# RMSNorm with SiLU on one core: all transfers in one queue, in turns of loads and of stores

## The chip, the cores and the metric

The kernel runs on one of the eight cores of a Trainium2 chip; the other cores do nothing. The metric is the device time of one execution, in microseconds (us), from three runs. One further execution was recorded by the hardware profiler; all durations below come from that one.

A core has a matrix engine (TensorE, PE in the profile), a vector engine (VectorE, DVE), a scalar engine for pointwise functions (ScalarE, ACT), GpSimd (POOL) and SyncE (SP), which computes nothing and issues transfers. Transfers between the main memory (HBM) and the on-chip memory (SBUF, 128 partitions) are carried out by 16 DMA engines. A transfer is issued by an instruction on SP or on ACT, and each of the two has its own queue to those 16 engines. A transfer instruction first waits in its engine's order for whatever it needs (data computed, a buffer free), and only then goes into the queue.

## The reference

```python
def setup_inputs():
    batch, seq_len, hidden = 8, 1024, 2048
    return {
        "x": np.random.randn(batch, seq_len, hidden).astype(np.float32),
        "gamma": np.random.randn(hidden).astype(np.float32),
        "eps": np.float32(1e-5),
    }

def reference(x, gamma, eps):
    rms = np.sqrt(np.mean(x ** 2, axis=-1, keepdims=True) + eps)
    out = gamma * x / rms
    return (out * (1 / (1 + np.exp(-out)))).astype(np.float32)
```

There are 8192 rows of 2048 float32 numbers: 67.1 MB are read and 67.1 MB written.

## The kernel before

The 8192 rows are cut into 16 blocks of 512 rows. A block is a tile `xt` of 128 partitions by 4 rows (`J = 4`) of 2048, 32 KB per partition and 4.19 MB in all, and each partition's 4 rows lie next to each other in HBM, so a block is one contiguous piece of HBM (`xb`, `ob`, lines 35 and 36) and each of its 128 runs is 32 KB long. There are six such tiles (`BUFS = 6`). A block is changed in place and stored from the tile it was loaded into, so the load of block b + 6 needs the store of block b to have landed.

Per block the work is:

- squares: for each row, the sum of squares. ScalarE does some rows (`squares_scalar`, line 65, Square with a running sum), VectorE the rest (`squares_vector`, line 73). Normally they take two rows each; for the even blocks from 4 to 12 ScalarE takes one and VectorE three (`share`, line 77). The squares themselves go to PSUM tiles that nobody reads.
- `root` (line 82): ScalarE takes the root of the mean plus eps for the 4 rows. Its function needs a table load, and SiLU later needs another.
- `invert` (line 87): VectorE, the reciprocal.
- `multiply` (line 92): VectorE, x times the row's factor times gamma, four instructions, one for each row.
- `silu` (line 98): ScalarE, SiLU in place, two instructions of two rows each, and then the store (line 102).

The last block goes another way: VectorE multiplies by gamma alone (line 155) and the row's factor enters as the scale of ScalarE's SiLU (line 157), row by row.

The instructions keep the order in which the program writes them, engine by engine (`manual_schedule`). Gamma is loaded into one partition and spread to all 128 by eight matmul instructions (line 113) and a copy (line 115). For blocks 0 to 2 (`SOON`) and at the end, the multiplications of a block stand ahead of the squares of the next; in between, the squares of block b + 1 come first.

Two queues carry the transfers. Every load is issued by ACT (line 54): those of blocks 0 and 1 at once, those of 2 to 5 behind a small copy on ACT that waits for gamma (line 116), and from then on the load of block b + 3 stands behind the first square of block b + 1. Gamma and every store are issued by SP, a store when its block's SiLU is done. So from the first store on, loads and stores are in flight side by side.

Of the kernel before, what the change touches and what calls it, by code (L numbers as in the profile page):

```python
# [1 line left out]

# [4 lines left out]

ACT = mybir.ActivationFunctionType
ALU = mybir.AluOpType


@with_exitstack
def kernel(
    ctx: ExitStack,
    tc: tile.TileContext,
    x: bass.AP,
    gamma: bass.AP,
    eps: bass.AP,
    out: bass.AP,
):  # L20

    nc = tc.nc
    P = nc.NUM_PARTITIONS
    f32 = mybir.dt.float32
    x2 = x.flatten_outer_dims()
    o2 = out.flatten_outer_dims()  # L30
    n, d = x2.shape
    J = 4
    BUFS = 6
    nblk = n // (P * J)
    xb = x2.rearrange("(b p j) d -> b p (j d)", p=P, j=J)
    ob = o2.rearrange("(b p j) d -> b p (j d)", p=P, j=J)

    singles = ctx.enter_context(tc.tile_pool(name="singles", bufs=1))
    pool = ctx.enter_context(tc.tile_pool(name="pool", bufs=BUFS))
    small = ctx.enter_context(tc.tile_pool(name="small", bufs=2))  # L40
    psum = ctx.enter_context(tc.tile_pool(name="psum", bufs=1, space=bass.MemoryType.PSUM))

    Q = 4
    w = d // Q
    g = singles.tile([P, d], f32)
    eps_t = singles.tile([P, 1], f32)
    ones = singles.tile([P, P], f32)
    junk_a = psum.tile([P, d], f32, name="junk_a")
    junk_v = psum.tile([P, d], f32, name="junk_v")
    blocks, sss, rmss, rstds = {}, {}, {}, {}  # L50

    def load(b):
        xt = pool.tile([P, J * d], f32, name="xt")
        nc.scalar.dma_start(out=xt, in_=xb[b])  # L54
        blocks[b] = xt

    def row(b, j):
        return blocks[b][:, j * d:(j + 1) * d]

    def squares_scalar(b, loads=()):  # L60


        sss[b] = small.tile([P, J], f32, name="ss")
        for j in range(share(b)):
            nc.scalar.activation(out=junk_a, in_=row(b, j), func=ACT.Square,  # L65
                                 accum_out=sss[b][:, j:j + 1])
            if j == 0:
                for s in loads:
                    load(s)

    def squares_vector(b):
        for j in range(share(b), J):
            nc.vector.tensor_tensor_reduce(  # L73
                out=junk_v, in0=row(b, j), in1=row(b, j), scale=1.0, scalar=0.0,
                op0=ALU.mult, op1=ALU.add, accum_out=sss[b][:, j:j + 1])

    def share(b):
        return 1 if 4 <= b <= 12 and b % 2 == 0 else 2

    def root(b):  # L80
        rms = small.tile([P, J], f32, name="rms")
        nc.scalar.activation(out=rms, in_=sss.pop(b), func=ACT.Sqrt, scale=1.0 / d, bias=eps_t)  # L82
        rmss[b] = rms

    def invert(b):
        rstd = small.tile([P, J], f32, name="rstd")
        nc.vector.reciprocal(out=rstd, in_=rmss.pop(b))  # L87
        rstds[b] = rstd

    def multiply(b):  # L90
        for j in range(J):
            nc.vector.scalar_tensor_tensor(out=row(b, j), in0=row(b, j), scalar=rstds[b][:, j:j + 1],  # L92
                                           in1=g, op0=ALU.mult, op1=ALU.mult)

    def silu(b):
        for h in range(0, J, 2):
            cols = slice(h * d, (h + 2) * d)
            nc.scalar.activation(out=blocks[b][:, cols], in_=blocks[b][:, cols], func=ACT.Silu)  # L98
        store(b)

    def store(b):
        nc.sync.dma_start(out=ob[b], in_=blocks[b])

    with tc.manual_schedule():

        load(0)
        nc.vector.memset(ones, 1.0)  # L107
        nc.vector.memset(eps_t, float(eps))
        nc.scalar.activation(out=junk_a[:, 0:1], in_=ones[:, 0:1], func=ACT.Square)  # L109
        nc.sync.dma_start(out=g[0:1, :], in_=bass.AP(tensor=gamma.tensor, offset=gamma.offset, ap=[[d, 1], [1, d]]))  # L110
        for c in range(Q):
            cols = slice(c * w, (c + 1) * w)
            nc.tensor.matmul(junk_v[:, cols], ones[0:1, :], g[0:1, cols], start=True, stop=True)  # L113
        load(1)
        nc.vector.tensor_copy(out=g, in_=junk_v)  # L115
        nc.scalar.copy(out=junk_a[:, 0:1], in_=junk_v[:, d - 1:d])  # L116
        for b in range(2, BUFS):
            load(b)

        last = nblk - 1
        SOON = 3
        squares_scalar(0)
        squares_vector(0)
        root(0)
        invert(0)
        for b in range(last):
            loads = [b + 3] if BUFS <= b + 3 < nblk else []
            if b < SOON:  # L130
                multiply(b)
                squares_scalar(b + 1, loads)
                silu(b)
                squares_vector(b + 1)
                root(b + 1)
            elif b < last - 1:
                squares_scalar(b + 1, loads)
                squares_vector(b + 1)
                root(b + 1)
                multiply(b)  # L140
                silu(b)
            else:
                multiply(b)
                squares_scalar(b + 1)
                silu(b)
                squares_vector(b + 1)
                root(b + 1)
            if b + 1 < last:
                invert(b + 1)


        for j in range(J):
            if j == J // 2:
                invert(last)
            nc.vector.tensor_mul(out=row(last, j), in0=row(last, j), in1=g)  # L155
        for j in range(J):
            nc.scalar.activation(out=row(last, j), in_=row(last, j), func=ACT.Silu,  # L157
                                 scale=rstds[last][:, j:j + 1])
        store(last)


# [1 line left out]
_INS = ['x', 'gamma', 'eps']  # L163
_OUTS = [((8, 1024, 2048), 'float32')]

_NUMBERS = {'eps': 9.999999747378752e-06}


# [26 lines left out]
```

## Time and profile before

| what | value |
|---|---|
| time, median of 3 runs | 317.0 us (316.79 to 317.33) |
| span of the profiled execution | 315.1 us |
| VectorE busy | 235.3 us, 75% of the span |
| ScalarE busy | 213.9 us, 68% |
| TensorE busy | 7.2 us, 2% |
| loads: 16 issues of 4096 KB | median 38.7 us from issue to landing |
| stores: 16 issues of 4096 KB | median 29.0 us from issue to landing |
| SP waiting for SiLU (line 98) ahead of a store | 271.4 us in 15 waits, the longest 22.2 |
| VectorE's squares waiting for a load | 42.2 us in 11 waits |

The span runs from the first to the last instruction of the profiled execution; the times of the runs include what lies around it. In the profile a group's row has the line, the engine, the operation, what is written from what, the shapes and the count, and behind the bars the busy time in us, the mean of one in ns, the idle time of the engine just before these instructions and what ended it. A row on a stretch of time has its start and end, its length, each engine's busy time, the clock, and last the busy share of the 16 DMA engines and the GB/s they moved. A DMA packet is counted where it starts, so short stretches can show a share over 1. The page's digits are tenths in 40 equal slices of 7.88 us.

### The profile page before, as it was taken

What the parts mean: (1) busy time and instruction counts of PE and PEld (TensorE: products, weight loads), DVE (VectorE), ACT (ScalarE), POOL (GpSimd) and SP (SyncE); (2) the same over time, 40 slices, a digit from 0 to 9 for tenths busy, and PEclk for the clock granted to TensorE, in tenths of its full rate; (3) what the DMA queues carried; (4) which work ended last, traced back from release to release, by engine and by line L of the source; (5) the groups of instructions that cost most, each with busy time, mean ns of one, the idle gap of its engine ahead of it and who ended that gap; (6) DMA issues with size and microseconds to landing.
All of it is one profiled execution on the core that took longest, in us unless ns stands there. A gap on an engine that the chain in (4) does not pass through costs nothing.

```text
span 315.1 us, 439 instructions
## 1 busy us (share of the span) xinstructions
PE 7.2 (2%) x8; PEld 2.5 (1%) x8; DVE 235.3 (75%) x157; ACT 213.9 (68%) x137; POOL 0.2 (0%) x4
## 2 busy tenths in 40 slices
PE   6200000000000000000000000000000000000000
PEld 2000000000000000000000000000000000000000
DVE  0679697979895695957969489593995939999600
ACT  1269998972799258682687827877278768779910
POOL 0000000000000000000000000000000000000000
DMA  8999999999999999999999999999999999999997
GB/s 334 412 453 416 383 458 408 462 403 462 403 459 408 454 412 458 408 462 403 462 403 462 408 458 408 458 408 458 416 449 416 449 416 449 428 437 428 437 428 308
DMA packets 4613, 134.24 MB, mean 426 GB/s; under 512 B 514, under 2 KB 514, under 8 KB 514
## 3 DMA queue, kind: packets, MB, share of 16 engines
q10 hardware_dynamic: 2304, 67.11, 49.8%
q1 hardware_dynamic: 2306, 67.12, 49.3%
q14 instruction: 3, 0.02, 0.0%
HBM read 67.12 MB, written 67.11 MB: 426 GB/s over the span
## 4 chain that ended last, share of the span: by engine, by line
DMA 68%; DVE 14%; ACT 11%; issue 1%; ACTq 1%; DVEq 0%
DMA xt<-in_x_dram 68%; DVE xt L92 9%; DVE junk_v L73 5%; ACT xt L98 4%; ACT junk_a L65 3%; ACT xt L157 2%; ACT L82 1%; ACTq L190 1%; ACT L157 0%; ACT L98 0%; ACT rms L82 0%; DVE ss L73 0%; ACTq L54 0%; DVE rstd L87 0%; ACT L109 0%
## 5 line engine op out<-in xcount | busy, mean ns | idle before, releaser
L92 DVE SCALAR_TENSOR_TENSOR xt<-xt,rstd,g 128x2048 f32<-128x2048 f32 x60 | 137.0, 2346 | 0.1
L98 ACT ACTIVATE xt<-xt 128x4096 f32<-128x4096 f32 x30 | 108.3, 3615 | 27.4 <-DVE xt L92 27.4
L73 DVE CUSTOM_DVE_ANT_0 junk_v<-xt 128x2048 f32<-128x2048 f32 x37 | 85.1, 2299 | 42.9 <-DMA xt<-in_x_dram 42.2
L65 ACT ACTIVATE junk_a<-xt 128x2048 f32<-128x2048 f32 x27 | 50.7, 1876 | 16.1 <-DMA xt<-in_x_dram 14.0
L82 ACT ACT_TABLE_LOAD x15 | 19.2, 1283 | 26.6 <-DVE ss L73 26.5
L98 ACT ACT_TABLE_LOAD x14 | 18.0, 1283 | 0.2
L115 DVE COPY g<-junk_v 128x2048 f32<-128x2048 f32 x1 | 2.3, 2292 | 9.0 <-PE junk_v L113 9.0
L87 DVE RECIPROCAL rstd<-rms 128x4 f32<-128x4 f32 x16 | 2.7, 172 | 8.4 <-ACT rms L82 8.4
L155 DVE TENSOR_TENSOR xt<-xt,g 128x2048 f32<-128x2048 f32 x4 | 8.9, 2277 | 0.0
L82 ACT ACTIVATE rms<-ss,eps_t 128x4 f32<-128x4 f32 x16 | 4.8, 297 | 5.7 <-DVE ss L73 5.5
L157 ACT ACTIVATE xt<-xt,rstd 128x2048 f32<-128x2048 f32 x4 | 7.7, 1991 | 0.0
L113 PE MATMUL junk_v<-g,ones 1*128 1x512 f32 x8 | 7.2, 1072 | 2.8 <-DMA g<-in_gamma_dram 2.8
L116 ACT COPY junk_a<-junk_v 128x1 f32<-128x1 f32 x1 | 0.1, 144 | 9.8 <-DVE g L115 9.8
L73 DVE DVE_READ_ACCUMULATOR2_ANT ss<- 128x1 f32 x37 | 5.2, 141 | 0.0
L65 ACT ACTIVATION_READ_ACCUMULATOR junk_a<-xt 128x1 f32 x27 | 5.0, 186 | 0.0
L113 PEld LDWEIGHTS junk_v<-g,ones 1*128 1x128 f32 x8 | 2.5, 325 | 5.9 <-issue 5.9
L109 ACT ACT_TABLE_LOAD x1 | 1.3, 1283 | 1.1 <-PEq L176 1.1
L157 ACT ACT_TABLE_LOAD x1 | 1.3, 1283 | 0.0
L107 DVE MEMSET ones<- 128x128 f32 x1 | 0.2, 165 | 0.8 <-PEq L176 0.8
L109 ACT ACTIVATE junk_a<-ones 128x1 f32<-128x1 f32 x1 | 0.2, 174 | 0.0
L176 POOL MEMSET const-bfloat16-1.0<- 128x1 bf16 x1 | 0.1, 103 | 0.0
L176 POOL MEMSET const-uint8-127<- 128x1 uint8 x1 | 0.1, 102 | 0.0
(3 smaller groups left out, 0.3 us busy)
## 6 DMA issues: line engine op xcount, KB each, us to landing
xt<-in_x_dram ACTq DMA_DIRECT2D x16, 4096.0 KB, 38.7
out_dram<-xt SPq DMA_DIRECT2D x16, 4096.0 KB, 29.0
g<-in_gamma_dram SPq DMA_DIRECT2D x1, 8.0 KB
```

The source lines that it names most:

```text
L65: nc.scalar.activation(out=junk_a, in_=row(b, j), func=ACT.Square, accum_out=sss[b][:, j:j + 1])
L73: nc.vector.tensor_tensor_reduce(out=junk_v, in0=row(b, j), in1=row(b, j), scale=1.0, scalar=0.0, op0=ALU.mult, op1=ALU.add, accum_out=sss ...
L82: nc.scalar.activation(out=rms, in_=sss.pop(b), func=ACT.Sqrt, scale=1.0 / d, bias=eps_t)
L87: nc.vector.reciprocal(out=rstd, in_=rmss.pop(b))
L92: nc.vector.scalar_tensor_tensor(out=row(b, j), in0=row(b, j), scalar=rstds[b][:, j:j + 1], in1=g, op0=ALU.mult, op1=ALU.mult)
L98: nc.scalar.activation(out=blocks[b][:, cols], in_=blocks[b][:, cols], func=ACT.Silu)
L109: nc.scalar.activation(out=junk_a[:, 0:1], in_=ones[:, 0:1], func=ACT.Square)
L113: nc.tensor.matmul(junk_v[:, cols], ones[0:1, :], g[0:1, cols], start=True, stop=True)
L115: nc.vector.tensor_copy(out=g, in_=junk_v)
L155: nc.vector.tensor_mul(out=row(last, j), in0=row(last, j), in1=g)
L157: nc.scalar.activation(out=row(last, j), in_=row(last, j), func=ACT.Silu, scale=rstds[last][:, j:j + 1])
L190: with _tile.TileContext(nc) as tc:
```

## The change

All 32 block transfers are issued by SP, in an order written out by hand (`QUEUE`). It alternates between turns of one direction: 6 blocks in, 5 out, 5 in, 5 out, 5 in, 6 out. Gamma's load moves from SP's queue to ACT's; the small copy of line 116 goes.

The six tiles become one tile `ring` with six slots, block b in slot b % 6. Two neighbouring blocks 2q and 2q + 1 now share their stretch of HBM: of the 8 rows that lie next to each other, a partition takes the first 4 for the even block and the last 4 for the odd one (`view`). So a single block has 128 runs of 32 KB, spaced by 64 KB, and a pair taken in one transfer has 128 runs of 64 KB. Pairs are taken in one transfer four times: the load of 4 and 5, and the stores of 0 and 1, 6 and 7, 10 and 11. A paired store waits for the SiLU of both.

`transfers(done)` issues the list's next entries for as long as they are loads or stores of blocks up to `done`. SP itself waits, in this order, for whatever each entry needs.

The compute order follows the turns (`GROUPS`: blocks 0 to 5, 6 to 10, 11 to 15). In the middle of a group the squares of block b + 1 come ahead of the multiplications of block b; a group's last block (but for the very last) is squared only after the multiplications and SiLU of the one before. ScalarE and VectorE now take two rows of squares each in every block.

```diff
+QUEUE = [
+    ('L', 0), ('L', 1), ('L', 2), ('L', 3), ('L', 4, 5),
+    ('S', 0, 1), ('S', 2), ('S', 3), ('S', 4),
+    ('L', 6), ('L', 7), ('L', 8), ('L', 9), ('L', 10),
+    ('S', 5), ('S', 6, 7), ('S', 8), ('S', 9),
+    ('L', 11), ('L', 12), ('L', 13), ('L', 14), ('L', 15),
+    ('S', 10, 11), ('S', 12), ('S', 13), ('S', 14), ('S', 15),
+]
+
+GROUPS = [range(0, 6), range(6, 11), range(11, 16)]
...
-    BUFS = 6
+    SLOTS = 6
...
-    xb = x2.rearrange("(b p j) d -> b p (j d)", p=P, j=J)
-    ob = o2.rearrange("(b p j) d -> b p (j d)", p=P, j=J)
...
-    pool = ctx.enter_context(tc.tile_pool(name="pool", bufs=BUFS))
-    small = ctx.enter_context(tc.tile_pool(name="small", bufs=2))
+    small = ctx.enter_context(tc.tile_pool(name="small", bufs=3))
...
+    ring = singles.tile([P, SLOTS * J * d], f32, name="xt")
...
-    def load(b):
-        xt = pool.tile([P, J * d], f32, name="xt")
-        nc.scalar.dma_start(out=xt, in_=xb[b])
-        blocks[b] = xt
+    def rows(b, j, k):
+        at = (b % SLOTS) * J + j
+        return ring[:, at * d:(at + k) * d]
...
+    def view(t, blocks):
+
+        q = blocks[0] // 2
+        both = t[q * 2 * P * J:(q + 1) * 2 * P * J, :].rearrange("(p j) d -> p (j d)", p=P, j=2 * J)
+        at = blocks[0] % 2 * J
+        return both[:, at * d:(at + len(blocks) * J) * d]
+
+    todo = list(QUEUE)
+
+    def transfer():
+        kind, *blocks = todo.pop(0)
+        sb = rows(blocks[0], 0, len(blocks) * J)
+        if kind == "L":
+            nc.sync.dma_start(out=sb, in_=view(x2, blocks))
+        else:
+            nc.sync.dma_start(out=view(o2, blocks), in_=sb)
+
+    def transfers(done):
+
+        while todo and (todo[0][0] == "L" or todo[0][-1] <= done):
+            transfer()
...
-    def share(b):
-        return 1 if 4 <= b <= 12 and b % 2 == 0 else 2
+    def squares(b):
+        squares_scalar(b)
+        squares_vector(b)
+        root(b)
...
-        store(b)
-
-    def store(b):
-        nc.sync.dma_start(out=ob[b], in_=blocks[b])
+            nc.scalar.activation(out=rows(b, h, 2), in_=rows(b, h, 2), func=ACT.Silu)
+        transfers(b)
...
-        load(0)
+        transfer()
...
+        nc.scalar.dma_start(out=g[0:1, :], in_=bass.AP(tensor=gamma.tensor, offset=gamma.offset, ap=[[d, 1], [1, d]]))
...
-        nc.sync.dma_start(out=g[0:1, :], in_=bass.AP(tensor=gamma.tensor, offset=gamma.offset, ap=[[d, 1], [1, d]]))
...
-        load(1)
+        transfer()
         nc.vector.tensor_copy(out=g, in_=junk_v)
-        nc.scalar.copy(out=junk_a[:, 0:1], in_=junk_v[:, d - 1:d])
-        for b in range(2, BUFS):
-            load(b)
...
+        transfers(-1)
+
+        for group in GROUPS:
+            first, end = group[0], group[-1]
+            squares(first)
+            invert(first)
+            multiply(first)
+            squares_scalar(first + 1)
+            silu(first)
+            squares_vector(first + 1)
+            root(first + 1)
+            for b in group[1:-1]:
+                if b + 1 < end or end == last:
+                    squares(b + 1)
+                invert(b)
                 multiply(b)
                 silu(b)
...
+            if end < last:
+                squares(end)
+                invert(end)
+                multiply(end)
+                silu(end)
...
-        store(last)
+        transfers(last)
```

## The prediction

> **What bounds the kernel now.** I read the page's DMA rows first, because a kernel that reads 67 MB, writes 67 MB and does little arithmetic is likely to be held by its transfers.
>
> ```profile
> span 315.1 us, 439 instructions
> DMA  8999999999999999999999999999999999999997
> GB/s 334 412 453 416 383 458 408 462 403 462 403 459 408 454 412 458 408 462 403 462 403 462 408 458 408 458 408 458 416 449 416 449 416 449 428 437 428 437 428 308
> DMA packets 4613, 134.24 MB, mean 426 GB/s; under 512 B 514, under 2 KB 514, under 8 KB 514
> q10 hardware_dynamic: 2304, 67.11, 49.8%
> q1 hardware_dynamic: 2306, 67.12, 49.3%
> ```
>
> The DMA digits are 9 in all slices but the first and the last, and the two queues together occupy 99.1% of the 16 engines' time (q10 is the loads, q1 the stores and gamma). So the span is bytes divided by rate, plus the two ends. The GB/s digits swing because a packet of 32 KB is counted whole where it starts. To see the rate I asked for longer stretches, cut where the traffic changes: start, loads alone, the first store's arrival, loads and stores together, stores alone, end. The last two columns are the share of the DMA engines and GB/s.
>
> ```profile
> 0.00:1.70 1.70, 0.00 (x0) 0.00 (x0) 0.17 (x2) 0.56 (x1) 0.20 (x4) 1.00 0.03 5
> 1.70:3.40 1.70, 0.62 (x1) 0.49 (x2) 0.00 (x0) 0.90 (x2) 0.00 (x0) 1.00 1.03 308
> 3.40:36.00 32.60, 6.54 (x8) 1.99 (x6) 20.95 (x14) 18.97 (x15) 0.00 (x0) 1.00 1.01 434
> 36.00:40.00 4.00, 0.00 (x0) 0.00 (x0) 3.17 (x3) 3.96 (x5) 0.00 (x0) 1.00 1.09 377
> 40.00:280.00 240.00, 0.00 (x0) 0.00 (x0) 194.53 (x129) 168.71 (x105) 0.00 (x0) 1.00 1.00 433
> 280.00:310.33 30.33, 0.00 (x0) 0.00 (x0) 16.46 (x11) 20.79 (x13) 0.00 (x0) 1.00 1.00 433
> ```
>
> This is the central reading. Loads alone run at 434 GB/s, loads and stores interleaved at 433, stores alone at 433. Mixing the directions, which the change stops, costs nothing here. At 433 GB/s the 134.24 MB take 310.0 us (the rounding of 433 is worth 0.4), and a block of 4.19 MB 9.69 us.
>
> What is left are two places where packets are long. At 1.70 to 3.40 the engines are busy 1.03 × 1.70 = 1.75 us at 308/1.03 = 299 GB/s, so 1.75 × (1 − 299/433) = **0.54 us** is lost while the first packets fill the path. At 36 to 40, where the first store joins (it is issued at 35.18), they are busy 1.09 × 4 = 4.36 us at 377/1.09 = 346 GB/s: 4.36 × (1 − 346/433) = **0.88 us** lost. Sum: 1.70 idle before the first load packet, 0.54, 0.88 and 310.0 make 313.1; the remaining 2.0 us to 315.1 are the last landing, the closing and the rounding. The profiled span stands 1.9 us below the median of 317.0; I take that as fixed and add it to every span.
>
> The compute engines' rows give the prices needed below; at 235 and 214 us busy neither VectorE nor ScalarE is the bound.
>
> ```profile
> L92 DVE SCALAR_TENSOR_TENSOR xt<-xt,rstd,g 128x2048 f32<-128x2048 f32 x60 | 137.0, 2346 | 0.1
> L98 ACT ACTIVATE xt<-xt 128x4096 f32<-128x4096 f32 x30 | 108.3, 3615 | 27.4 <-DVE xt L92 27.4
> L73 DVE CUSTOM_DVE_ANT_0 junk_v<-xt 128x2048 f32<-128x2048 f32 x37 | 85.1, 2299 | 42.9 <-DMA xt<-in_x_dram 42.2
> L82 ACT ACT_TABLE_LOAD x15 | 19.2, 1283 | 26.6 <-DVE ss L73 26.5
> L82 ACT ACTIVATE rms<-ss,eps_t 128x4 f32<-128x4 f32 x16 | 4.8, 297 | 5.7 <-DVE ss L73 5.5
> L155 DVE TENSOR_TENSOR xt<-xt,g 128x2048 f32<-128x2048 f32 x4 | 8.9, 2277 | 0.0
> ```
>
> **The change, part by part.**
>
> *Bytes and start.* All 67.11 MB each way stay: 310.0 us at 433 GB/s. The first load is issued by SP instead of ACT; both queues issue their first transfer at 0.73 in the trace, so the 1.70 and the 0.54 stay. Gamma changes places with it on ACT's queue; ACT has only its table load behind it. The L116 copy, which held the loads of blocks 2 to 5 back to 12.4 us, goes; since 434 GB/s flow across that point, its removal is worth 0.
>
> *One queue instead of two.* In the new list SP waits on each store's SiLU and on each slot's earlier store, in order, and everything behind it in the list waits too. This costs nothing as long as the DMA queue still holds issued transfers. The stock at each point: loads 0 to 5 end at 1.70 + 0.54 + 6 × 9.69 = 60.4. The pair of stores 0,1 needs SiLU of block 1. The trace has that block's squares and root done by 36.8; the new order puts block 2's squares, root and table load on ACT before SiLU (about 2 × 2.03 + 0.30 + 2 × 1.28 = 6.9, to 43.7), while VectorE does two squares (2 × 2.4) and four multiplies (9.14) from 34.0 to about 48.1; the second SiLU half of 3.6 ends it at 51.7. **Margin 8.7 us.** In the second group, block 6 lands near 119 (60.4 + 5 stores + itself = 118.5, and 0.5 to land); squares 4.8, root, table load and inverse 1.8, multiplies 9.14, squares of 7 and 8 9.6, multiplies 9.14, SiLU 3.6 give 157.1 for the pair 6,7, against 60.4 + 11 × 9.69 = 167.0, when loads 6 to 10 and store 5 are through. **Margin 9.9 us.** In the third, block 11 lands near 215.9 (22 blocks); the same chain without the pair's second multiply, with ScalarE's own order, reaches SiLU of 11 at about 238, against 60.4 + 20 × 9.69 = 254.2. Margin 16. The last store: from 215.9 VectorE has 10 squares × 2.4, 16 multiplies × 2.29, 4 × 2.24 and one 1.8 wait = 71.4, to 287.3, and two last SiLU rows (2 × 1.9) make 291, against 60.4 + 25 × 9.69 = 302.7. Margin 11. Loads that wait for a store: load 10 waits for store 4 (landed at about 109.4) with loads 6 to 9, 38.8 us of work, in front of it; load 15 likewise. So no turn runs dry, and the compute order (GROUPS, the dropped `share`) costs 0 under this cover. If cover failed, the price is the shortfall plus a refill: 0.97 from issue to first packet (0.73 to 1.70) and 0.54.
>
> *The first store's stretch.* 0.88 us were lost when a second queue joined a running one. In the new kernel the first store follows in a queue that is already running. Bounds: 0 (it belongs to the store, and stays) to 0.88 gained. The only other such stretch, 0.54, is also a queue that starts; later stores begin on a queue with work left (29.0 us median from issue to landing against 9.69 of work) and the stretch from 40 on shows no loss. Nearer to that: I take **−0.9**.
>
> *Five turns of direction inside one queue.* No row shows one. Bounds: the stretch 40 to 280, where 433 GB/s flow while each engine's packets alternate between queues, gives 0 per turn; the one entry of a new direction gives 0.88. A gain below zero is excluded by 434 for loads alone. The alternating stretch has thousands of changes of direction and the entry one, so I take **0** each and keep 5 × 0.88 = 4.4 for the range.
>
> *64 KB runs.* Four pairs × 128 partitions merge 512 packets: 32 fewer on each of 16 engines, and 4 fewer completions. The nearest row is the completion packet of 4 B, 9 ns in the DMA records: at most 36 × 9 ns = 0.32 gained, 0 if a run is still cut at 32 KB; middle: **−0.15**. That blocks 4 and 5 land together delays block 4's squares by 9.69, inside the margins above (store 4 is ready near 89, needed at 98.5).
>
> The Trainium skill, DMA: Bandwidth & Descriptors, section "Why small descriptors are slow (HBM only)", gives about 3 cycles per packet beside one cycle per 32 B; on that, an estimate of the merged packets' gain is 3 of 2051 cycles on a quarter of the bytes, near 0.1 us, inside my bounds. A rule on the same page speaks against the change: "Latency and other measured facts" has rates falling with power-of-two row pitch in HBM (207 against 214 GB/s per direction at 512 KiB). The change doubles the pitch of the 32 KB runs from 32 to 64 KB; no row here shows a wider pitch, and if that 3% held for the 24 unpaired blocks, an estimate from the page is 0.033 × 0.75 × 310 = 8 us more.
>
> **Sum**: 315.1 − 0.9 − 0.15 + 0 = 314.05 of span, and with 1.9, **316.0 us**.
>
> **The rivals.**
>
> 1. *The stretch moves with the first store.* For: both lossy places come where bytes first go a new way. Against: the other one has loads alone. Then only the 64 KB gain is left: 317.0 − 0.15 = 316.85, within what can be told from no change.
> 2. *Each turn costs what the first store cost* (slower). Between two queues, one queue's next packet is ready while the other's finishes; in one queue a write stands directly behind a read, and the pipe may fill anew. For: the only first change of direction shown cost 0.88. Against: 433 in the alternating stretch. At the full price 317.0 − 0.88 − 0.15 + 5 × 0.88 = 320.4. It decides from 5t > 0.9 + 0.15 + 0.63, t = 0.34 us a turn.
> 3. *A turn runs dry*: the ring is one tile, and if its slots were ordered as a whole, or a margin of 8.7 were eaten, SP would issue late. For: SP's long waits in the old trace were for SiLU, and loads now stand behind them. Against: the margins, and rows of one old tile were already told apart (SiLU of two rows starts before the other two are multiplied). One refill on every turn is 5 × (0.97 + 0.54) = 7.6: 323.5, more with a shortfall.
>
> **How the numbers follow.** My forecast has 0.47, the moved stretch 0.24, costly turns 0.22, a dry queue 0.07. A difference of 0.2% (0.63 us) is about what a measurement of this kernel can tell from no change. Faster (below 316.4): 0.47, the forecast. Same: rival 1, and 0.03 of rival 2 with cheap turns, 0.27. Slower: 0.19 and 0.07, 0.26. The forecast's own range is 315.3 to 316.4: the full 64 KB gain (−0.17), the runs' scatter (316.79 to 317.33), and the rounding. The range reaches to turns of 0.53 us each (317.0 − 1.05 + 2.65 = 318.6), leaving out the dear half of rival 2, the dry queue and a little below: 0.19.
>
> **What would show it.** One queue with 4096 − 512 large packets and a DMA digit of 9 throughout; 433 GB/s in stretches inside a turn; no loss at the first turn near 60 us (at 0.88 there alone, rival 1; at all five, near 60, 109, 157, 206 and 254, rival 2); SP waiting long for SiLU while the DMA stays busy, where a GB/s dip with SP waiting would be rival 3. I am wrong in the main step if loads alone or stores alone, held for 50 us, do not run at 433, or if the wider pitch slows them.

## The result, and the profile after

The changed kernel takes 317.5 us (median of 21 runs, 317.16 to 317.92) against 316.98 for the kernel before beside it (21 runs, 316.75 to 317.33): ratio 1.0017, interval 1.0011 to 1.0023. It is half a microsecond slower, a small loss but clear of the scatter, where 316.0 was forecast.

The page of the changed kernel, its DMA rows:

```profile
span 315.9 us, 420 instructions
DMA  8999999999899999999999999999999999999996
DMA packets 4036, 134.24 MB, mean 425 GB/s; under 512 B 449, under 2 KB 449, under 8 KB 449
q1 hardware_dynamic: 4032, 134.22, 98.9%
q10 hardware_dynamic: 2, 0.01, 0.0%
```

The change does what it says: one queue carries everything, in 4036 packets instead of 4613, and the engines are still busy throughout. One slice (79 to 87 us) shows an 8. Packets of 64 KB, counted where they start, blur such digits, so here are stretches cut by turn (start, end, length, busy time of each engine, clock, and last the DMA share and GB/s):

```profile
1.70:3.40 1.70, 0.72 (x1) 0.50 (x2) 0.00 (x0) 1.03 (x2) 0.00 (x0) 1.00 1.06 313
56.00:64.00 8.00, 0.00 (x0) 0.00 (x0) 6.68 (x4) 7.96 (x5) 0.00 (x0) 1.00 0.79 279
64.00:110.00 46.00, 0.00 (x0) 0.00 (x0) 35.59 (x23) 36.18 (x21) 0.00 (x0) 1.00 1.00 433
110.00:157.00 47.00, 0.00 (x0) 0.00 (x0) 34.01 (x23) 30.09 (x23) 0.00 (x0) 1.00 1.00 432
254.00:312.00 58.00, 0.00 (x0) 0.00 (x0) 34.90 (x23) 37.53 (x23) 0.00 (x0) 1.00 1.00 433
```

A turn of stores runs at 433 GB/s, a later turn of loads at 432, as the interleaved stretch did before. The loss is again in one place, 56 to 64 us, where the first store follows the first six loads. The reading is that of the forecast: busy 0.79 × 8 = 6.32 us at 279/0.79 = 353 GB/s, so 6.32 × (1 − 353/433) = **1.17 us** lost. The kernel before lost 0.88 at its first store.

SP's waits, by line (L79 issues the loads, L81 the stores; who waited, for whom, us in total, times, longest):

```profile
SPq L81 <- ACT xt L122: 181.1, 11, 28.5
SPq L79 <- DMA out_dram<-xt: 42.6, 6, 9.4
```

SP waited long for SiLU and for stores to land, and it cost nothing, since the queue was stocked: the DMA share is 1.00 in the turns shown above. Its issues show the compute order met the forecast's chain (start, duration over all, count):

```profile
51.02 38.74 SPq L81 DMA_DIRECT2D out_dram<-xt  x4
89.81 21.91 SPq L79 DMA_DIRECT2D xt<-in_x_dram  x5
240.20 52.53 SPq L81 DMA_DIRECT2D out_dram<-xt  x5
```

The first pair of stores is issued at 51.0 (51.7 was worked out), the third turn of stores begins to be issued at 240.2 (238).

One more thing sets the end, and no stretch shows it: the 16 engines do not finish together. Each block transfer has 16 completion counts in the trace, which are read here as one for each engine. For the last store, in us:

```
                         first engine   mean     last engine
kernel before               313.46      313.78     314.29
changed kernel              313.50      314.00     314.85
```

On the mean the changed kernel ends 0.22 later, its last engine 0.56 later; its span ends 1.0 after that landing, where before it was 0.86. So of the 0.7 us between the two profiled spans (315.15 and 315.86), 0.22 are work that all engines share, 0.34 the spread between them, 0.15 the closing.

The 0.34 are one execution of each kernel and can't be put down to the change. The last engine ends 0.82 us behind the mean in the kernel before with one small store more (a run below), and 0.49 in the changed kernel with the same store. As far as the times tell, much of the spread comes from a fetch of instructions: 8 KB on queue q14, which takes one DMA engine 309 ns, with a longer data packet beside it. In the changed kernel the last engine is 0.37 behind the mean at the load that lands at 62.5 us and 0.78 behind at the store that lands at 82.3. Between the two, at 71.5, lies a fetch, and the data packet beside it is 357 ns longer, 0.67 us together.

### The profile page after: what moved, and what is told of

It reads as the page before. It is cut to its first block, busy times and chain, and to the rows that moved or that the text cites. A ratio compares the mean times of both kernels' runs of the same rounds, so it can differ in the third digit from the quotient of the medians.

```text
span 315.9 us, 420 instructions
## 1 busy us (share of the span) xinstructions
PE 7.2 (2%) x8; PEld 2.5 (1%) x8; DVE 224.4 (71%) x147; ACT 218.0 (69%) x142; POOL 0.2 (0%) x4
## 2 busy tenths in 40 slices
DMA packets 4036, 134.24 MB, mean 425 GB/s; under 512 B 449, under 2 KB 449, under 8 KB 449
## 4 chain that ended last, share of the span: by engine, by line
DVE 58%; DMA 25%; ACT 6%; issue 2%; DVEq 1%; ACTq 1%; another core or an unknown queue 0%; SPq 0%
DVE xt L117 37%; DMA xt<-in_x_dram 25%; DVE junk_v L96 19%; ACT xt L122 2%; ACT xt L165 2%; DVE xt L163 1%; ACT L107 1%; DVEq L198 1%; DVE ss L96 1%; ACTq L198 1%; DVE rstd L112 0%; ACT rms L107 0%; SPq L81 0%; ACTq L107 0%
## 5 line engine op out<-in xcount | busy, mean ns | idle before, releaser
L96 DVE CUSTOM_DVE_ANT_0 junk_v<-xt 128x2048 f32<-128x2048 f32 x32 | 73.5, 2298 | 40.2 <-DMA xt<-in_x_dram 39.6
L91 ACT ACTIVATE junk_a<-xt 128x2048 f32<-128x2048 f32 x32 | 60.0, 1876 | 50.6 <-DMA xt<-in_x_dram 50.1
L91 ACT ACTIVATION_READ_ACCUMULATOR junk_a<-xt 128x1 f32 x32 | 6.0, 186 | 0.0
L96 DVE DVE_READ_ACCUMULATOR2_ANT ss<- 128x1 f32 x32 | 4.5, 140 | 0.0
```

Source lines behind the costliest of these rows:

```text
L96: nc.vector.tensor_tensor_reduce(out=junk_v, in0=row(b, j), in1=row(b, j), scale=1.0, scalar=0.0, op0=ALU.mult, op1=ALU.add, accum_out=sss ...
```

## The experiments

Each ratio is to runs of the kernel before on the same chip (its medians there were 316.8 to 316.9), with its 95% interval.

**Without the pairs.**

```diff
-    ('L', 0), ('L', 1), ('L', 2), ('L', 3), ('L', 4, 5),
-    ('S', 0, 1), ('S', 2), ('S', 3), ('S', 4),
+    ('L', 0), ('L', 1), ('L', 2), ('L', 3), ('L', 4), ('L', 5),
+    ('S', 0), ('S', 1), ('S', 2), ('S', 3), ('S', 4),
...
-    ('S', 5), ('S', 6, 7), ('S', 8), ('S', 9),
+    ('S', 5), ('S', 6), ('S', 7), ('S', 8), ('S', 9),
...
-    ('S', 10, 11), ('S', 12), ('S', 13), ('S', 14), ('S', 15),
+    ('S', 10), ('S', 11), ('S', 12), ('S', 13), ('S', 14), ('S', 15),
```

> The changed kernel with its four paired transfers taken apart into single blocks of 32 KB runs; order, queue and pitch stay. If the first store's stretch grows with the 64 KB packet that it falls on (1.2 us in the profile after against 0.9 before), the stretch shrinks by 0.3 and the 64 KB gain of some 0.3 us (512 packets of 65 KB at 2418 ns against twice 1213 on 16 engines, 0.26) is given back: 317.5 within 0.2. If the pairs cost nothing and only gain, 317.8. If the pairs are what made the changed kernel slower (a skew between the engines that large packets bring), 317.0 or less.

317.37 us, 1.0015 (1.0006 to 1.0023). The stretch did not shrink:

```profile
56.00:64.00 8.00, 0.00 (x0) 0.00 (x0) 7.97 (x6) 7.96 (x5) 0.00 (x0) 1.00 0.91 332
```

7.28 busy at 365 GB/s is 1.14 us lost, against 1.17 with pairs. So the long stretch is not the 64 KB packet's. The completion counts of the last store average 314.12 here and 314.00 with pairs: that is 0.12 less with pairs, but two profiles of one kernel (contiguous blocks, below) differ by 0.10 there, at 313.77 and 313.87. In the times no gain shows.

**A small store ahead of everything**, in the changed kernel on ACT's queue and in the kernel before on SP's, each behind gamma's load:

```diff
+        nc.scalar.dma_start(out=o2[0:16, 0:P], in_=ones[0:16, :])
```

```diff
+        nc.sync.dma_start(out=o2[0:16, 0:P], in_=ones[0:16, :])
```

> The changed kernel with one small store more: 16 partitions of 512 B each, issued on ACT's queue right behind gamma, to a place of the output that block 0 writes again later. Theory: the loss of about 1 us near 60 us belongs to the first store of each DMA engine, whatever its size and queue; then it moves to the first 3 us, where the path is being filled anyway, the stretch near 58 is gone, and the time is 316.4 to 317.0. Rival: the loss belongs to the turn from loads to stores of whole blocks, or to the queue of the first store; then it stays near 58 and the time is 317.5 or a little more (0.1 for the packets).

> The kernel before with the same small store, issued on SP's queue behind gamma. Theory of the first store: the loss at 36 to 40 (0.9 us by the share of the DMA engines) goes, 316.0 to 316.6. Rival (a second queue that joins a running one with block transfers): the loss stays at 36 and the time is 317.0.

317.36, 1.0019 (1.001 to 1.0028), and 317.05, 1.0002 (0.9994 to 1.0011). The theory that the loss belongs to the first store whatever its size falls: the stretch stays where it was in both. For the changed kernel, then for the one before:

```profile
56.00:64.00 8.00, 0.00 (x0) 0.00 (x0) 6.82 (x4) 7.96 (x5) 0.00 (x0) 1.00 0.83 295
```

```profile
36.00:40.00 4.00, 0.00 (x0) 0.00 (x0) 3.19 (x3) 3.96 (x5) 0.00 (x0) 1.00 1.09 393
```

Losses of 1.19 and 0.73 us by the same sum.

**A larger early store**, 8 KB from each of 16 partitions to 16 places 512 KB apart:

```diff
+        nc.vector.memset(rows(5, 0, 1), 0.0)
...
+        nc.scalar.dma_start(out=o2[0:1024, :].rearrange("(p k) d -> p k d", k=64)[:, 0, :], in_=rows(5, 0, 1)[0:16, :])
```

> The changed kernel with a larger early store: 16 rows of 8 KB, one for each DMA engine, each to its own 512 KB of the first pair's output, which is written again later; issued by ACT about 4 us in, from a slot that VectorE has set to 0, and the load of blocks 4 and 5 waits for it. It costs 16 packets of 8 KB, about 0.3 us. If the stretch belongs to an engine's first store of some size or to the place it writes to, it goes from 58 us and the time is 316.6 to 317.1. If it belongs to the first whole block that is stored, it stays at 58 and the time is 317.5 to 317.9.

317.69, 1.0026 (1.0016 to 1.0035). The stretch stays (1.27 us lost), and the 0.3 us of the store's own packets (309 ns on each engine) come on top:

```profile
56.00:64.00 8.00, 0.00 (x0) 0.00 (x0) 6.75 (x4) 7.96 (x5) 0.00 (x0) 1.00 1.03 377
```

The loss comes where the first whole block is stored, and neither of these two stores takes it away.

The records of single packets in the traces say more: the lost time stands in load packets. In the kernel before, 31 load packets (queue q10) that start between 36.19 and 38.36 us take 0.07 to 0.85 us more than the usual 1213 ns, while the store's first packets (q1, from 39.61 on) take 1213. In the changed kernel it is 16 packets of 64 KB, which start at 57.9 to 58.4 and take 0.8 to 1.5 us more than the usual 2418 ns: in order of start the last 16 load packets ahead of the first store. Without pairs it is the last 32 (0.51 and 0.61 us for each engine).

**The layout.** In one queue without pairs, blocks as contiguous pieces again (run twice); and in the kernel before, the wide pitch alone:

```diff
-        q = blocks[0] // 2
-        both = t[q * 2 * P * J:(q + 1) * 2 * P * J, :].rearrange("(p j) d -> p (j d)", p=P, j=2 * J)
-        at = blocks[0] % 2 * J
-        return both[:, at * d:(at + len(blocks) * J) * d]
+        return t.rearrange("(b p j) d -> b p (j d)", p=P, j=J)[blocks[0]]
```

```diff
-    xb = x2.rearrange("(b p j) d -> b p (j d)", p=P, j=J)
+    xb = [x2[b // 2 * 2 * P * J:(b // 2 + 1) * 2 * P * J, :].rearrange("(p j) d -> p (j d)", p=P, j=2 * J)[:, b % 2 * J * d:(b % 2 + 1) * J * d] for b in range(nblk)]
```

(the same for `ob`)

> The changed kernel without pairs and with the old layout (each block one contiguous piece of HBM): what is left is one queue in turns and the compute order. If the wider pitch of 64 KB costs anything, this is faster than the version without pairs (317.37); if not, it is the same within 0.2. If one queue in turns is by itself what costs (a longer stretch at the first store, 1.1 us against 0.9, and engines that drift apart without being brought together), it stays at 317.2 to 317.5 and does not come back to 316.9.

> The version with contiguous blocks and no pairs once more, on this chip beside the others. If its gain over the version without pairs (317.06 against 317.37) is the layout's, it is 316.9 to 317.2 again, with a stretch of 0.6 to 0.9 us near 58. If it was chance, 317.3 to 317.5 and a stretch of 1.1 or more.

> The kernel before with only the layout changed: runs of 32 KB spaced by 64 KB, two queues as they were. If the pitch is innocent 316.9 within 0.2 and 433 GB/s in the long stretch; if a wider pitch slows the transfers as the page on DMA has it for 512 KB (3%), up to 10 us more.

One queue, contiguous: 317.06, 1.0014 (1.0004 to 1.0024), and 317.15, 1.0009 (1.0001 to 1.0018). The stretch is much shorter, in the first of the two:

```profile
56.00:64.00 8.00, 0.00 (x0) 0.00 (x0) 7.97 (x6) 7.96 (x5) 0.00 (x0) 1.00 0.99 393
```

0.99 × 8 busy at 397 GB/s, 0.66 us lost (0.75 in the second). The kernel before with the wide pitch: 316.96, 1.0007 (0.9998 to 1.0015), 433 GB/s from 40 to 280 us, 0.96 lost at 36 to 40:

```profile
36.00:40.00 4.00, 0.00 (x0) 0.00 (x0) 3.33 (x3) 3.96 (x5) 0.00 (x0) 1.00 1.11 377
40.00:280.00 240.00, 0.00 (x0) 0.00 (x0) 194.55 (x129) 168.71 (x105) 0.00 (x0) 1.00 1.00 433
```

So the pitch does not slow the transfers; what differs with it, in one queue, is the one-off loss at the first store.

**Only the first blocks contiguous**, and the first paired store taken apart:

```diff
+        if blocks[0] < 4:
+            return t.rearrange("(b p j) d -> b p (j d)", p=P, j=J)[blocks[0]]
```

> The changed kernel with blocks 0 to 3 in the old layout (contiguous blocks) and the first paired store taken apart, so that the first stores go to one contiguous piece; all later blocks and the other three pairs stay. Theory: the part of the loss that depends on the layout falls at the first store alone. Then the stretch near 58 is 0.6 to 0.8 us instead of 1.2 and the time is that of the contiguous version or a little less by the three pairs, 316.8 to 317.1. Rival (the layout costs at every turn, or the profiled stretch differs from run to run by itself): 317.3 to 317.5.

317.25, 1.0014 (1.0005 to 1.0023). The stretch fell, to 7.12 us busy at 382 GB/s, 0.84 lost, a little above the expected 0.6 to 0.8; the time lies between the two expectations and does not decide. **A pitch of 128 KB**:

```diff
-        q = blocks[0] // 2
+        q = blocks[0] // 4
...
-        at = blocks[0] % 2 * J
+        at = blocks[0] % 4 * J
```

(and four blocks in the view instead of two)

> The changed kernel without pairs and with four blocks sharing their stretch of HBM, so that the 32 KB runs of a block are spaced by 128 KB. If the stretch at the first store grows with the pitch (0.66 us at 32 KB, 1.15 at 64), it is 1.4 us or more here and the time 317.6 or more. If only contiguous against not contiguous counts, 1.1 to 1.2 and 317.4. If the two profiles differed by chance, anything from 0.7 to 1.2 and 317.0 to 317.4.

317.61, 1.0022 (1.0013 to 1.0031), but with a loss of only 0.80 at the first store:

```profile
56.00:64.00 8.00, 0.00 (x0) 0.00 (x0) 7.97 (x6) 7.96 (x5) 0.00 (x0) 1.00 0.98 381
```

This speaks against a loss that grows with the pitch. The long time of this run has another look: the last store's completions run from 313.45 to 315.20, mean 313.92, so the last engine ends 1.3 us behind the mean. Over all profiles of one queue, the loss at the first store is 1.17, 1.14, 1.19, 1.27 and 1.16 at a pitch of 64 KB, 0.66 to 0.84 in the six with contiguous first blocks (those below included), and 0.80 at 128 KB. These runs were spread over several chips, and that is a rival which no run settles: on the chip of the 128 KB run, contiguous first blocks gave 0.72 to 0.84 and a pitch of 64 KB was not tried. Only one chip is known to have had both layouts in one queue, with 1.27 (the larger early store) against 0.66.

**Two queues in the new order**, stores issued by ACT behind their SiLU:

```diff
-            nc.sync.dma_start(out=view(o2, blocks), in_=sb)
+            nc.scalar.dma_start(out=view(o2, blocks), in_=sb)
```

> The changed kernel with its stores issued by ACT, right behind each SiLU; loads stay on SP, pairs, pitch, slots and compute order stay. Loads now start as soon as their slot is free, so the directions mix again. If the single queue is what made the changed kernel slower, this comes back to the time before or below it by the pairs' gain: 316.6 to 317.0, with a stretch of 0.7 to 0.9 us at the first store. If the pairs, the pitch or the compute order did it, it stays near 317.5.

334.52, 1.0563 (1.0547 to 1.0579): neither. The compute order made for turns does not feed mixed queues, and the engines stand idle near the end:

```profile
285.00:295.00 10.00, 0.00 (x0) 0.00 (x0) 4.15 (x2) 6.86 (x5) 0.00 (x0) 1.00 0.60 256
295.00:305.00 10.00, 0.00 (x0) 0.00 (x0) 9.93 (x9) 7.43 (x6) 0.00 (x0) 1.00 0.61 262
```

At shares of 0.60 and 0.61 some 8 us are lost in these 20. For the time it is no test of the single queue; it shows what the cover that the forecast counted is worth once it is gone. Its first store does tell something: the loss there, from 50 to 58 us, is 1.38 us (1.08 of share at 393 GB/s) where 0.7 to 0.9 was expected. So with the pitch and the pairs the loss is large in two queues as well.

**Shorter turns**, one compute group, single blocks. Turns of one, with the wide pitch and contiguous:

```diff
+    ('S', 0),
+    ('S', 1),
+    ('L', 6),
+    ('S', 2),
+    ('L', 7),
...
-GROUPS = [range(0, 6), range(6, 11), range(11, 16)]
+GROUPS = [range(0, 16)]
```

> One queue, single blocks, pitch as in the changed kernel, but the direction changes after every block once the first six are in: 21 changes of direction instead of 5, and one compute group. If a turn is free (what the forecast took), the time is that of the changed kernel without pairs, 317.6 within 0.3. If a turn costs t, it is 16 t more: at 0.1 us a turn 319.2, at 0.88 a turn 331.

> Turns of one block in one queue, as in the run with 21 changes of direction that took 320.99, but with contiguous blocks. If the loss at a change of direction comes from the wide pitch, it goes: 317.0 to 317.5, with landings of the last store no more than about 1 us apart on the 16 engines. If it belongs to the change of direction in one queue, it stays: 320 to 322, landings 4 us apart.

320.99, 1.0127 (1.0113 to 1.0141), and 320.9, 1.0123 (1.011 to 1.0137). So a change of direction in one queue is not free as such, and the layout has no part in it. The DMA engines are busy throughout; the packets' records of the contiguous one show where: around each change from loads to stores (89, 109, 128, 148, 167 us and so on), packets of up to 1213 ns + 0.56 us (a single one + 0.9), hardly one at the changes back. Summed over the packets that are more than 60 ns too long, after 64 us and without 0.03 for two instruction fetches, that is 1.55 us on the mean engine, 0.155 for each of the ten later changes. The time grows by more, since the losses do not fall evenly on the engines, as the landings show. Completions of the last store, in us:

```
                              first engine   mean     last engine
one queue, contiguous            313.38      313.77     314.40
turns of one, contiguous         314.24      315.28     318.16
turns of two, contiguous         313.54      314.30     315.80
```

Turns of two and of three, contiguous:

> Contiguous blocks, one queue, turns of two blocks: 11 changes of direction, against 21 in the run that took 320.9 and 5 in the contiguous version (317.06 and 317.15). If each change costs the same (3.8 us for 16 more, 0.24 each), 6 more make 318.6. If the loss depends on how short the turn is, so that only turns of one pay, 317.1 to 317.5.

> The same with turns of three: 9 changes of direction. At 0.24 us for each change 318.1; if only short turns pay, 317.1 to 317.4.

Turns of two: 319.4, 1.007 (1.0053 to 1.0087), with runs from 317.38 to 319.49, and in the profiled run (318.44) 0.12 us on the mean engine for each later change to stores. It speaks for a price at every such change, and the median is even above the 318.6 that an equal price gave. Turns of three: 328.02, 1.0352 (1.0337 to 1.0367), but not for their turns. The stock ran out, as rival 3 had it:

```profile
280.00:290.00 10.00, 0.00 (x0) 0.00 (x0) 3.35 (x3) 3.35 (x3) 0.00 (x0) 1.00 1.00 426
290.00:300.00 10.00, 0.00 (x0) 0.00 (x0) 9.96 (x7) 7.14 (x6) 0.00 (x0) 1.00 0.38 164
300.00:310.00 10.00, 0.00 (x0) 0.00 (x0) 9.45 (x6) 8.52 (x4) 0.00 (x0) 1.00 0.53 226
```

Block 15 is loaded alone in a last turn, behind three stores, so its squares come late and everything after it waits; 62% and 47% of two stretches of 10 us are idle. This run's time doesn't price a turn. Its packet records show how uneven the price is: under 0.01 us on the mean engine at the first two of the later changes to stores, 0.17 and 0.15 at the last two.

In the changed kernel the same sum of long packets after 64 us is 0.037, of which 0.03 is the two instruction fetches (an 8 KB packet each, 309 ns, near 71 and 95 us; the kernel before has them near 89 and 109). So its two later changes to stores cost under 0.01 on the mean engine, against 0.03 each in the contiguous version and 0.095 at one of the two with only the first blocks contiguous. Why a change to stores after five blocks costs so much less than after one or two stays open.

## Why the prediction was wrong

**The bound, the rates and the cover: right.** The transfers set the time in both kernels, loads and stores alone run at 432 to 433 GB/s, no turn ran dry, and the compute order, with the two chains checked above right to within about 2 us, cost nothing. (By the prediction's own terms store 4 is needed at 60.4 + 4 × 9.69 = 99.2, not 98.5; nothing hangs on it.) What can happen without that cover, two of the experiments show: 8 us and more of idle engines.

**The first store's stretch: the step that failed.** The forecast took "−0.9", reasoning that the loss came from a second queue joining a running one. It stayed in the single queue and was 1.17, so this term is +0.3 instead of −0.9, 1.2 of the 1.5 us between the forecast's 316.0 and the 317.5 measured. That is rival 1, held at 0.24, and more: rival 1 would have given 316.85. The failed inference was from two places where a queue starts to a cause in the queue. The start of the run and the first store have a second thing in common, which the rival named, and nothing that the prediction read in the old trace told the two apart. What the prediction named as proof that its main step was wrong, other rates or a costly pitch, did not come, and this step failed all the same. The runs show what the loss is not: not the second queue, not the 64 KB packet, not an engine's first store of 512 B or 8 KB. In one queue it is larger by some 0.4 us in the five profiles with the 64 KB pitch than in the six with contiguous first blocks. That the pitch makes it larger is likely, not shown: 128 KB gave 0.80, and the chips differ. Why the last load packets ahead of the first whole store take longer stays open.

**Five turns at 0: nearly right for this kernel, wrong as a rule.** Beside the first, the later changes to stores cost under 0.01 each on the mean engine. Packets of the later load turns were a few ns longer than 1213: on all large packets after 64 us these small excesses sum to 0.16 us per engine, against 0.04 before. That is a term of 0.1 that the sum had not. The reasoning from interleaved queues to a single queue was wrong: in one queue, with turns of one or two, each change from loads to stores cost 0.085 to 0.155 on the mean engine. In the time, turns of one cost 320.9 − 317.1 = 3.8 us over 16 changes more than in the contiguous version, 0.24 for each change in either direction, which is how rival 2 counts. That is short of the 0.34 from which rival 2 said it would decide, and the changed kernel's later changes cost far less. The range's bound of 0.88 held for these.

**64 KB runs at −0.15: inside its bounds, its size not settled.** By the packets' durations a merged packet saves 8 ns (2418 against twice 1213), 0.26 us on each engine, and with four completions of 9 ns fewer 0.29, near the upper bound of 0.32. The mean landings differ by 0.12, hardly more than two profiles of one kernel do, and in the time there is no gain (317.37 without pairs, 317.50 with).

**The engines' spread: outside the sum.** The forecast added up mean losses. The end is the last engine's, which was 0.51 us behind the mean before, 0.85 in the changed kernel and 2.9 in turns of one. Between the first two the difference of 0.34 is not shown to be the change's (0.82 and 0.49 with the small store ahead, the other way round); in turns of one the spread grows from change to change. Landings show that the spread, once there, mostly stays: from first to last engine 1.19 us for the store that lands at 82 us, 1.35 for the last one.

The 0.22 by which the mean landing is later do not close to the last tenth: the stretch gives +0.3, small excesses and long packets +0.13, fewer packets and completions −0.29 by their durations, and the first load lands 0.06 earlier (12.59 against 12.65). That makes 0.1; the other 0.1 is not traced.

The Trainium skill's figures on row pitch (DMA: Bandwidth & Descriptors, "Latency and other measured facts") start at 512 KiB. The prediction's estimate from the page carried them down to 64 KB, where they would have made 8 us; the kernel before with that pitch ran at 433 GB/s and 316.96 us, so there is no such loss at 64 KB. The same page's fixed 3 cycles per packet ("Why small descriptors are slow (HBM only)") gave an estimate of near 0.1 us for the pairs; by the records' 8 ns for a merged packet it is 0.26.

How the half microsecond divides by median times: one queue, turns and order alone +0.2 (317.06 and 317.15), the wide pitch some +0.25 (317.37), the pairs +0.1 (317.50). The intervals of neighbours overlap, and by the ratios to the kernel before on the same chip (1.0014 and 1.0009, then 1.0015, then 1.0017) the steps are smaller still, so this division is likely at most, not shown. No version was faster than the kernel before.

## What to carry to other kernels

When the DMA engines are busy for 99% of the span at one rate in every direction, an order of transfers has only the losses at a few places to gain, and each must be traced to its cause before it is booked as a gain; two places that look alike are not a cause. Count the end by the last of the 16 engines, not by the mean. Changing direction block by block in one queue can cost several microseconds with the engines busy all the time, and a hand-written turn order is safe only as long as each waiting store has work in front of it.

## What the runs showed of the hardware

- Where the first whole block is stored, 0.7 to 1.4 us are lost on the mean engine, in one queue or two, and a small store ahead of it doesn't take it away. The lost time stands in the last load packets ahead of the store's first ones.
- In one queue with turns of one or two blocks, a change from loads to stores costs 0.085 to 0.155 us on the mean engine, a change from stores to loads hardly anything, and the last store's completions come up to 4.5 us apart.
- An 8 KB instruction fetch takes one DMA engine 309 ns of its own time, and a data packet that starts 0.3 us later is longer by 113 to 357 ns; two such fetches explain the only long packets (1569 and 1328 ns) in the steady part of the kernel before. Around one such fetch (309 + 357 ns) the last engine of the changed kernel went from 0.37 to 0.78 us behind the mean.
